# A two-block transformer kernel on one core: joined norm and logarithm steps, and fp32 one-hot products made as two fp32r parts

## The chip, the cores and the metric

The kernel runs on one core of one Trainium2 chip. The metric is the device time of one execution in microseconds (us), lower is better; several executions are timed and the median is given.

## The reference, cut to what matters

Two blocks are applied to one sequence of 256 tokens with 1024 features, all in float32. The first block runs four mixers side by side (latent attention, window means, a state-space scan, a gated recurrence), then a feed-forward part and a gated embedding. The second block has two layers: dilated attention or stick-breaking attention, each with a layer norm, a mixture of 16 experts (two per token) and another layer norm. What the change touches is this:

```python
# rmsnorm, used everywhere in the first block
y = x * rsqrt(mean(x * x, -1) + 1e-6) * g
# state-space scan: decays from running sums of a, per head
a_cs = cumsum(a, -1);  lmat = exp(segsum(a))      # segsum: a_cs[l] - a_cs[s]
# dilated attention: relative bias, a row of a 32 x 16 table per distance
bias = table[rel_bucket(dist)]
# stick-breaking attention, per head: z clipped to +-60
#   weight(i, j) = exp(z_ij - sum over j <= k < i of log(1 + exp(z_ik)))
# layer norm at the end of each of the two layers
x = (x - mean) * rsqrt(var + 1e-5) * g + b
```

## The kernel before, in words

Everything is written for a scheduler that keeps data dependences and places the instructions on the engines' queues; each engine then works its queue in order. Weights arrive by DMA on the SP queue in pieces of 128x1024 (`raw`). A piece is split into two fp32r parts: ScalarE copies it to `whi` (rounded), VectorE takes `wlo = raw - whi` (`wsplit`, L299 to L316). There are 4 buffers for each part, that is two weight pieces of 2048 columns. A projection is then three fp32r products per 128x128 weight block: `whi` by the high part of x, `whi` by its low part, `wlo` by the high part (`mm3`, called by `proj`, `proj_beside`, `proj_tok`). `sequence` and `later_pieces` list the pieces in the order of use; `piece(n)` hands out n of them and keeps one more converted ahead.

The parts that the change touches:

- `rstd` (L432): squares of x, two blocks of 128 features at a time, are added up, and a product with a matrix of ones sums over the 128 partitions. For 8 blocks the squares come as `tot` (blocks 0 to 5 added) and `sq` (the last two); with `halve` each of the two is folded to 256 columns first, so 2 products with plain fp32 operands are made; without it 4. It is called with `halve` at the start of the first block, and without it in `first_tail` (feed-forward and gated embedding) and in `dilated`.
- `rel_rows`: the rows of the relative bias come from a product of the 32x16 table with a one-hot matrix of 1152 columns, in three plain fp32 products of 384 columns.
- `ssd_dt` and `ssd`: the running sums `acs` (8 heads x 256 tokens) lie on 8 partitions; for each head a plain fp32 product with a column of the identity spreads one row over 128 partitions (8 products of 256 columns).
- `stick`: stick-breaking attention. `begin` makes the first query and key with `proj_beside`; per head `scores` clips z (`sbz`) and makes l = log(1 + exp z) (`sbl`) by Abs, Exp and Ln on ScalarE and three operations on VectorE; `sums` multiplies l (384 columns) with a triangle of ones and one 128-column part of it with ones, both in plain fp32. There are 16 heads, taken by pairs, and four quads of heads; the order of the steps is the list `steps`.
- `across_norm`: between the first expert stage and `stick`, 32 warm-up products, then 16 transposes, then per block of 128 features ScalarE makes the high part, VectorE the scaled x and the low part.
- `moe` and `token_norm`: after the last expert, the two halves of the tokens are each normed by a chain of small operations; in the second layer gain and offset rows follow and the four quarters of the output are stored.

Of the kernel before, what the change touches and what calls it, by code (L numbers as in the profile page):

```python
# [8 lines left out]
F32 = mybir.dt.float32  # L9
# [7 lines left out]
D = 1024  # L17
# [186 lines left out]
class Kern:  # L204
# [142 lines left out]
    def piece(self, n=1, beside=None):  # L347

        while len(self.made) < n + 1 and self.pieces:
# [3 lines left out]
        now, self.made = self.made[:n], self.made[n:]  # L353
        return now if n > 1 else now[0]
# [51 lines left out]
    def proj_beside(self, ws, kt, x, evacs, step):  # L406
# [3 lines left out]
        for k0 in range(0, kt, step):  # L410
# [21 lines left out]
    def rstd(self, x, nb, eps, dim, halve=False):  # L432
# [11 lines left out]
        if halve:  # L444
            for t in both:
                self.tt(t[:, 0], t[:, 0], t[:, 1], OP.add)
# [232 lines left out]
    def rel_rows(self):  # L679
# [3 lines left out]
        oh = A.tile([32, RELW], F32, name="bucket")  # L683
        nc.gpsimd.dma_start(oh, self.ap["bucket"])
# [135 lines left out]
    def first_tail(self, acc):  # L820
# [195 lines left out]
    def ssd_dt(self, src):  # L1016
# [19 lines left out]
        self.acs = A.tile([8, S], F32, name="acs")  # L1036
        nc.vector.tensor_copy(self.acs, ph[:8, :S])
        self.dtT = dt

    def ssd(self, xb):  # L1040
# [43 lines left out]
        def pair(hp):  # L1084
            o = self.ps("od")
            for s_ in range(2):
# [3 lines left out]
                self.mm(pr[:, :S], self.k["ident"][:8, h:h + 1].to_broadcast([8, 128]), self.acs, True, True)  # L1090
# [27 lines left out]
    def dtend(self):  # L1118
        t = self.A.tile([8, 8], F32, name="dend")
        self.ts(t, self.k["ident"][:8, :8], self.acs[:, 127:128], OP.mult)  # L1120
# [53 lines left out]
    def dilated(self, x, h):  # L1174
# [12 lines left out]
        def ev_q(quad, g):  # L1187
            def ev(j, p):
                nonlocal r
                if r is None:  # L1190
                    r = self.rstd(x, 8, 1e-6, D)
# [143 lines left out]
    def stick(self, x, h):  # L1335
        nc, A, ap = self.nc, self.A, self.ap
        self.table("natural_log_exp_and_others")
        self.later_pieces()
        at = self.new_split(8)
        tiles = {}  # L1340

# [6 lines left out]
        def begin():  # L1348
            self.proj_beside(self.piece(2), 8, h,
                             [ev("q", 0, 0.125), ev("k", 0, 1.0)], 2)  # L1350
# [10 lines left out]
        def scores(quad, hp):  # L1361
# [12 lines left out]
            for z, l in zip(zs, ls):  # L1374
# [6 lines left out]
            tiles["z", quad, hp] = zs, ls  # L1381

        def sums(quad, hp):

            for z, l in zip(*tiles["z", quad, hp]):
# [238 lines left out]
    def moe(self, layer, x):  # L1624
# [116 lines left out]
        def down(i, hs):  # L1741
# [4 lines left out]
            wd = wsp[1] if i == 8 else self.beside([ap["e_d"][layer, 2 * i + s] for s in range(2)], 2048)  # L1746
# [55 lines left out]
        self.raws, self.turn = raws, -1  # L1802
        across(7)
        back(*ys.pop(0), False, False)
        y = down(*prev)
# [6 lines left out]
    def token_norm(self, layer, xr, acc, along):  # L1812
# [5 lines left out]
        for n, c in enumerate(cols):  # L1818
            for t in range(2):
# [3 lines left out]
                self.act(sq, xr[:, t, c], AF.Square, accum_out=sqs[:, t, n:n + 1])  # L1823
        for t in range(2):
            o = slice(t, t + 1)
            self.tt(nm[:, o], sums[:, t, 0:1], sums[:, t, 1:2], OP.add)
            self.tt(rs[:, o], sqs[:, t, 0:1], sqs[:, t, 1:2], OP.add)
            self.ts(nm[:, o], nm[:, o], -1.0 / D, OP.mult)
            self.tt(u[:, o], nm[:, o], nm[:, o], OP.mult)
            self.stt(rs[:, o], rs[:, o], 1.0 / D, u[:, o], OP.mult, OP.subtract)  # L1830
            self.act(rs[:, o], rs[:, o], AF.Sqrt, bias=self.eps[1e-5])
            nc.vector.reciprocal(rs[:, o], rs[:, o])
            self.tt(nmr[:, o], nm[:, o], rs[:, o], OP.mult)
            for n, c in enumerate(cols):
                if n:
# [3 lines left out]
                if along:  # L1839
                    self.tt(xr[:, t, c], xr[:, t, c], along[0][:, c], OP.mult)  # L1840
                    self.tt(xr[:, t, c], xr[:, t, c], along[1][:, c], OP.add)
                    nc.sync.dma_start(self.out[t * 128:t * 128 + 128, c], xr[:, t, c])
# [154 lines left out]
```

## Time and profile before

| | us |
|---|---|
| runs shown, median (lowest to highest of 3) | 1289.57 (1289.53 to 1291.12) |
| the profiled execution, its own time | 1292.46 |
| span of the profiled execution, first to last instruction | 1290.7 |
| TensorE (PE) busy | 1258.6 |
| VectorE (DVE) busy | 731.3 |
| ScalarE (ACT) busy | 610.2 |
| mean granted TensorE clock, share of full speed | 0.991 |

The profile lists, for each engine, what it did and how long it stood idle before, and what ended the idle time. PEld is the weight load of TensorE, which runs beside the products. The chain of waits follows the work that ended last back to the start. A plain fp32 product of TensorE shows as two records; an fp32r product as one. Records of TensorE overlap, so the distance from start to start is what a product costs in a row of products. In the span, the first block takes the time to about 545 us, dilated attention to about 838 us, the first expert stage and its norm to about 994 us, stick-breaking attention to about 1123 us, the second expert stage to about 1275 us, the last norm and the store the rest.

### The profile page before, as it was taken

The page shows a single profiled execution, that of the slowest core. Times are in us where ns is not written, and L with a number is a line of the kernel's source. Part 1 is how long each engine was busy: PE and PEld are TensorE (multiplying, and loading weights), DVE is VectorE, ACT ScalarE, POOL GpSimd, SP SyncE. Part 2 cuts the span into 40 slices and gives each one's busy share as a digit, 9 for nine tenths or more (in the row PEclk, how much of TensorE's full clock was granted, in tenths as well). Part 3 has the DMA queues.
Part 4 walks back from the last instruction along what each step waited for, and adds up shares of the span by engine and source line. Part 5 has one row for each costly group of instructions (what it writes and reads, how often), then busy time and mean ns, then how long its engine had stood idle before and what let it go on. Part 6 is the DMA issues. An engine that isn't in the chain of part 4 may idle for free.

```text
span 1290.7 us, 22672 instructions
## 1 busy us (share of the span) xinstructions
PE 1258.6 (98%) x9159; PEld 1043.3 (81%) x9159; DVE 731.3 (57%) x1416; ACT 610.2 (47%) x951; POOL 24.8 (2%) x48
## 2 busy tenths in 40 slices
PE   9999999999999999999999999999998999999995
PEld 7987899999999999999999999855334999754332
DVE  7877667558665545876464646263215677454214
ACT  6674666446544544755454545232115666242112
POOL 0000000000000000000000000002000000002000
PEclk9999999999999999999999999999999999999998
DMA  7452346657486555566464645599999444557893
GB/s 263 147 183 71 109 137 204 187 178 241 142 300 229 178 186 176 185 190 187 141 194 134 194 134 170 166 318 332 358 395 370 131 131 131 191 196 272 331 397 132
DMA packets 91105, 268.28 MB, mean 208 GB/s; under 512 B 26528, under 2 KB 26672, under 8 KB 90736
## 3 DMA queue, kind: packets, MB, share of 16 engines
q1 hardware_dynamic: 86576, 252.80, 58.5%
q0 software_dynamic: 4416, 13.94, 3.2%
q8 instruction: 74, 1.21, 0.4%
q14 instruction: 39, 0.32, 0.1%
HBM read 267.68 MB, written 6.89 MB: 213 GB/s over the span
## 4 chain that ended last, share of the span: by engine, by line
PE 86%; DVE 5%; DMA 4%; ACT 3%; issue 1%; SPq 0%; ACTq 0%; DVEq 0%
PE ps L250 54%; PE acc L250 14%; PE y L250 6%; PE sc L250 4%; PE o L250 2%; PE sd L250 1%; PE o L258 1%; ACT whi L236 1%; DVE wlo L239 1%; PE sc L1265 1%; DMA raw<-e_d 1%; PE tr L250 1%; DMA s<-rows 1%; DMA wlo<-e_gu 1%; DMA raw<-e_gu 1%
## 5 line engine op out<-in xcount | busy, mean ns | idle before, releaser
L250 PE MATMUL ps<-s,whi 128*128 128x256 f32 x2656 | 495.0, 286 | 5.3 <-DVE s L239 2.5
L239 DVE TENSOR_TENSOR wlo<-raw,whi 128x1024 fp32r<-128x1024 f32 x276 | 333.8, 1218 | 258.5 <-ACT whi L236 258.0
L236 ACT ACTIVATE whi<-raw 128x1024 fp32r<-128x1024 f32 x276 | 287.1, 1054 | 307.1 <-PE ps L250 222.9
L250 PEld LDWEIGHTS ps<-s,whi 128*128 128x128 f32 x2656 | 414.9, 190 | 12.3 <-DVE s L239 4.0
L250 PE MATMUL ps<-s,wlo 128*128 128x256 f32 x1328 | 378.2, 285 | 1.3 <-DVE wlo L239 1.3
L250 PEld LDWEIGHTS ps<-s,wlo 128*128 128x128 f32 x1328 | 251.0, 189 | 4.6 <-DVE wlo L239 2.6
L250 PE MATMUL acc<-hid,whi 128*128 128x256 f32 x512 | 93.0, 281 | 0.0
L250 PE MATMUL ps<-whi,s 128*128 128x256 f32 x512 | 92.3, 282 | 0.0
L250 PE MATMUL ps<-raw,xg 128*64 128x512 f32 x344 | 86.2, 597 | 0.0
L250 PEld LDWEIGHTS ps<-whi,s 128*128 128x128 f32 x512 | 78.2, 188 | 1.5
L250 PEld LDWEIGHTS acc<-hid,whi 128*128 128x128 f32 x512 | 79.3, 189 | 0.0
L250 PE MATMUL acc<-hid,wlo 128*128 128x256 f32 x256 | 72.3, 283 | 0.0
L250 PE MATMUL ps<-wlo,s 128*128 128x256 f32 x256 | 71.7, 280 | 0.0
L250 PEld LDWEIGHTS ps<-raw,xg 128*64 128x64 f32 x344 | 25.7, 136 | 43.9 <-issue 40.5
L236 ACT ACTIVATE eh<-ps 128x256 f32<-128x256 f32 x16 | 6.2, 385 | 114.9 <-PE ps L250 114.9
L247 DVE SCALAR_TENSOR_TENSOR eh<-ps,gslot,eh 128x256 f32<-128x256 f32 x16 | 7.7, 484 | 85.2 <-ACT eh L236 85.2
L236 ACT ACTIVATE s<-y 128x512 fp32r<-128x512 f32 x36 | 21.0, 597 | 69.2 <-PE y L250 69.2
L239 DVE TENSOR_TENSOR s<-y,s 128x512 fp32r<-128x512 f32 x36 | 24.3, 686 | 50.6 <-ACT s L236 50.4
L250 PEld LDWEIGHTS ps<-wlo,s 128*128 128x128 f32 x256 | 48.1, 188 | 0.0
L250 PE MATMUL acc<-s,whi 128*128 128x256 f32 x256 | 47.7, 286 | 0.3 <-ACT dprobT L236 0.3
L250 PEld LDWEIGHTS acc<-hid,wlo 128*128 128x128 f32 x256 | 47.9, 187 | 0.0
L250 PE MATMUL y<-raw,hs 128*64 128x512 f32 x180 | 46.7, 600 | 0.0
(407 smaller groups left out, 1748.9 us busy)
## 6 DMA issues: line engine op xcount, KB each, us to landing
raw<-e_gu SPq DMA_DIRECT2D x81, 512.0 KB, 7.9
raw<-w_dil SPq DMA_DIRECT2D x72, 512.0 KB, 4.6
raw<-w_ff SPq DMA_DIRECT2D x64, 512.0 KB, 4.7
raw<-e_d SPq DMA_DIRECT2D x43, 512.0 KB, 10.1
raw<-w_g SPq DMA_DIRECT2D x32, 512.0 KB, 4.0
whi<-e_gu SPq DMA_DIRECT2D x31, 512.0 KB, 8.4
raw<-w_a SPq DMA_DIRECT2D x28, 512.0 KB, 4.8
raw<-w_sb SPq DMA_DIRECT2D x24, 512.0 KB, 7.8
```

The lines of the kernel that those rows point to most:

```text
L236: return self.nc.scalar.activation(out, in_, func, **k)
L239: return self.nc.vector.tensor_tensor(out, a, b, op=op)
L247: return self.nc.vector.scalar_tensor_tensor(out, a, s, b, op0=op0, op1=op1, **k)
L250: self.last_mm = self.nc.tensor.matmul(out, l, r, start=first, stop=last, skip_group_check=True).ins,
L258: self.nc.tensor.matmul(p, self.ones_b, r, start=True, stop=True, skip_group_check=True)
L1265: nc.tensor.transpose(pt[:, c * 128:(c + 1) * 128], e[:, order[c]], self.k["ident"])
```

## The change

- `rstd` with `halve` first adds `sq` to `tot` and folds once, so one fp32 product stands where two stood; the calls in `first_tail` and `dilated` now use `halve` too.
- `rel_rows`, `ssd` and `sums` take the data operand in two fp32r parts (a rounded copy by ScalarE, the remainder by VectorE) and multiply each with the one-hot, triangle or ones matrix in fp32r. `l` has 2 buffers in place of 6, its parts 4 each, and the `half` tiles of this stage 3 in place of 4.
- `begin` of `stick` makes all products with the high part of x first, then those with the low part.
- `token_norm` works on both halves of the tokens at once; in the second layer the mean is taken off and the gain applied while the square root is made.
- `moe` issues the last expert's down weights before the last transposes, and the list of stick weights is filled there; `make(0)` converts none.

```diff
+    def make(self, n, beside=None):
+        while len(self.made) < n and self.pieces:
...
-    def proj_beside(self, ws, kt, x, evacs, step):
+    def proj_beside(self, ws, kt, x, evacs, step, second=False):
         out = [self.ps() for _ in ws]
-        for k0 in range(0, kt, step):
+        for part in (0, 1) if second else ():
+            for k0 in range(0, kt, step):
+                for w, p in zip(ws, out):
+                    for b in range(2):
+                        for k in range(k0, min(k0 + step, kt)):
+                            for i, xp in ((0, x.lo),) if part else ((0, x.hi), (1, x.hi)):
+                                self.mm(p[:, b * S:(b + 1) * S], self.cut(w[i], k * S + b * 128, 128), xp[:, k],
+                                        not part and i == 0 and k == 0 and b == 0, part == 1 and k == kt - 1)
+        for k0 in () if second else range(0, kt, step):
...
         if halve:
-            for t in both:
-                self.tt(t[:, 0], t[:, 0], t[:, 1], OP.add)
+            if len(both) > 1:
+                self.tt(tot, tot, both.pop(), OP.add)
+            self.tt(tot[:, 0], tot[:, 0], tot[:, 1], OP.add)
...
+        tb2 = A.tile([32, 2, 16], F32R, name="reltab2")
+        self.act(tb2[:, 0], tb, AF.Copy)
+        self.tt(tb2[:, 1], tb, tb2[:, 0], OP.subtract)
...
-            self.mm(p[:16, :384], tb, oh[:, c0:c0 + 384], True, True)
+            for i in range(2):
+                self.mm(p[:16, :384], tb2[:, i], oh[:, c0:c0 + 384], i == 0, i == 1)
...
-                rs.append(self.rstd(x, 8, 1e-6, D))
+                rs.append(self.rstd(x, 8, 1e-6, D, True))
...
-        self.acs = A.tile([8, S], F32, name="acs")
-        nc.vector.tensor_copy(self.acs, ph[:8, :S])
+        self.acs = [A.tile([8, S], F32R, name=f"acs{i}") for i in range(2)]
+        self.act(self.acs[0], ph[:8, :S], AF.Copy)
+        self.tt(self.acs[1], ph[:8, :S], self.acs[0], OP.subtract)
+        self.mid, self.pick8 = A.tile([8, 1], F32, name="acs_mid"), A.tile([8, 8], F32R, name="pick8")
+        nc.vector.tensor_copy(self.mid, ph[:8, 127:128])
+        nc.vector.tensor_copy(self.pick8, self.k["ident"][:8, :8])
...
-                self.mm(pr[:, :S], self.k["ident"][:8, h:h + 1].to_broadcast([8, 128]), self.acs, True, True)
+                for i, a in enumerate(self.acs):
+                    self.mm(pr[:, :S], self.pick8[:, h:h + 1].to_broadcast([8, 128]), a, i == 0, i == 1)
...
-            ls = [A.tile([128, 384], F32, name="sbl", bufs=6) for _ in ps]
+            parts = [[A.tile([128, 384], F32R, name=n, bufs=4) for n in ("sblh", "sbll")] for _ in ps]
+            ls = [A.tile([128, 384], F32, name="sbl", bufs=2) for _ in ps]
...
+                self.act(hi, l, AF.Copy)
+                self.tt(lo, l, hi, OP.subtract)
...
-                self.mm(pr[:, :384], self.k["suffix"], l, True, False)
-                self.mm(pr[:, 128:256], self.ones, l[:, 256:384], False, True)
+                for i, l in enumerate(parts):
+                    self.mm(pr[:, :384], suffix, l, i == 0, False)
+                    self.mm(pr[:, 128:256], ones, l[:, 256:384], False, i == 1)
...
+        wd = down_weights(prev[0])
+        if not layer:
+            self.later_pieces()
+            self.make(0)
         across(7)
         back(*ys.pop(0), False, False)
-        y = down(*prev)
+        y = down(*prev, wd)
...
+        self.tt(nm, sums[:, :, 0], sums[:, :, 1], OP.add)
+        self.ts(nm, nm, -1.0 / D, OP.mult)
+        def centre(t):
+            for c in cols:
+                self.stt(xr[:, t, c], xr[:, t, c], nm[:, t:t + 1], along[0][:, c], OP.add, OP.mult)
+        if along:
+            centre(0)
+        self.tt(u, nm, nm, OP.mult)
+        self.tt(rs, sqs[:, :, 0], sqs[:, :, 1], OP.add)
+        self.stt(rs, rs, 1.0 / D, u, OP.mult, OP.subtract)
+        self.act(rs, rs, AF.Sqrt, bias=self.eps[1e-5])
+        if along:
+            centre(1)
+        nc.vector.reciprocal(rs, rs)
...
+                if along:
+                    self.stt(xr[:, t, c], xr[:, t, c], rs[:, o], along[1][:, c], OP.mult, OP.add)
+                    nc.sync.dma_start(self.out[t * 128:t * 128 + 128, c], xr[:, t, c])
```

## Rows read from the trace of the kernel before

**Rows 1.** The page, parts 1 and 4: busy time, and the chain by engine.

```profile
PE 1258.6 (98%) x9159; PEld 1043.3 (81%) x9159; DVE 731.3 (57%) x1416; ACT 610.2 (47%) x951; POOL 24.8 (2%) x48
...
PE 86%; DVE 5%; DMA 4%; ACT 3%; issue 1%; SPq 0%; ACTq 0%; DVEq 0%
```

**Rows 2.** Windows: stretch, length, busy PE, PEld, DVE, ACT, POOL, clock, DMA, GB/s.

```profile
0.00:207.00 207.00, 199.91 (x1407) 175.77 (x1408) 150.18 (x353) 130.77 (x224) 5.59 (x22) 0.98 0.48 156
...
341.00:521.00 180.00, 180.00 (x1488) 177.99 (x1487) 100.08 (x114) 86.99 (x103) 1.81 (x4) 1.00 0.62 204
...
984.00:1012.00 28.00, 25.34 (x161) 19.87 (x159) 20.93 (x49) 20.00 (x32) 0.00 (x0) 0.94 0.60 231
...
1043.00:1067.00 24.00, 24.00 (x192) 21.73 (x190) 17.16 (x37) 16.19 (x27) 0.00 (x0) 1.00 0.41 132
...
1226.00:1275.00 49.00, 48.14 (x206) 19.84 (x202) 8.09 (x15) 8.40 (x16) 0.00 (x0) 1.00 0.85 326
```

**Rows 3.** The chain of waits in order of time: start, length, what, records.

```profile
529.31 1.73 PE acc L250 x8
...
607.35 1.75 PE sc L1265 x16
...
1024.29 1.73 PE sc L250 x8
1026.03 5.76 PE ps L250 x48
```

**Rows 4.** Timeline of PE in the feed-forward part: products of `rstd`.

```profile
335.55 1.03 PE L250 MATMUL acc<-half,ones 128*128 128x256 f32 x4
```

**Rows 5.** Products by tile: the relative bias, then the state-space rows.

```profile
L250 PE MATMUL ps<-bucket,reltab x6: 481/481/492, 342.5 to 361.4; 32*16 32x384 f32 x6
...
L250 PE MATMUL sd<-acs,consts x16: 374/426/478, 101.9 to 136.3; 8*128 8x256 f32 x16
```

**Rows 6.** Timeline of PE: fp32r products of 320 columns in an expert stage.

```profile
1178.47 1.33 PE L250 MATMUL y<-oneh,s 128*128 128x320 f32 x8
...
1180.23 1.33 PE L250 MATMUL y<-oneh,s 128*128 128x320 f32 x8
```

**Rows 7.** Groups by form: DVE and ACT on 128x384 tiles of stick-breaking attention.

```profile
L236 ACT ACTIVATE sbl<-sbl 128x384 f32<-128x384 f32 x32 | 15.8, 518 | 0.5
...
L247 DVE SCALAR_TENSOR_TENSOR sbl<-sbz,sbl 128x384 f32<-128x384 f32 x16 | 8.9, 555 | 10.9 <-ACT sbl L236 10.9
```

**Rows 8.** Timeline from the end of the first expert stage into stick-breaking attention.

```profile
984.70 7.08 PE L258 MATMUL tr<-ones_b 128*128 128x512 bf16 x32
...
994.51 0.38 PE L250 MATMUL ps<-s,whi 128*128 128x256 f32 x1
...
995.36 1.36 ACT L236 ACTIVATE s<-y,vecs 128x256 fp32r<-128x256 f32 x2
...
996.08 0.39 PE L250 MATMUL ps<-s,whi 128*128 128x256 f32 x1 [1.19 <-DVE s L239]
...
997.84 0.55 PE L250 MATMUL ps<-s,whi 128*128 128x256 f32 x1 [1.14 <-DVE s L239]
...
1001.69 0.42 DVE L239 TENSOR_TENSOR s<-x,s 128x256 fp32r<-128x256 f32 x1
...
1003.37 1.06 ACT L236 ACTIVATE whi<-raw 128x1024 fp32r<-128x1024 f32 x1 [1.86 <-PE ps L250]
...
1010.49 0.40 PE L250 MATMUL ps<-whi,s 128*128 128x256 f32 x2
```

**Rows 9.** Timeline from the last expert's sums to the end.

```profile
1274.61 0.69 DVE L1820 CUSTOM_DVE_ANT_0 x<-x,acc 128x512 f32<-128x512 f32 x1 [0.28 <-PE acc L250]
...
1279.27 2.50 DVE L239 TENSOR_TENSOR x<-x,s 128x512 f32<-128x512 f32 x4
...
1282.45 2.50 DVE L239 TENSOR_TENSOR x<-x,s 128x512 f32<-128x512 f32 x4
```

**Rows 10.** Waits from 984 to 1125 us: total, times, longest.

```profile
DVE wlo L239 <- ACT whi L236: 19.9, 17, 3.4
```

More of the change, by code (lines that the diff above doesn't have):

```diff
@@ L347, in piece @@
     def piece(self, n=1, beside=None):
-        while len(self.made) < n + 1 and self.pieces:
+        self.make(n + 1, beside)
+        now, self.made = self.made[:n], self.made[n:]
+        return now if n > 1 else now[0]
+    def make(self, n, beside=None):
+        while len(self.made) < n and self.pieces:
             src, width = self.pieces.pop(0)
@@ L1190, in ev @@
                 if r is None:
-                    r = self.rstd(x, 8, 1e-6, D)
+                    r = self.rstd(x, 8, 1e-6, D, True)
                     self.table("natural_log_exp_and_others")
@@ L1337, in stick @@
         self.table("natural_log_exp_and_others")
-        self.later_pieces()
+        if self.dense:
+            self.later_pieces()
         at = self.new_split(8)
         tiles = {}
+        suffix, ones = (A.tile([128, 128], F32R, name=n) for n in ("suffix_r", "ones_r"))
+        nc.vector.tensor_copy(suffix, self.k["suffix"])
+        nc.vector.tensor_copy(ones, self.ones)
         def ev(n, quad, scale):
@@ L1370, in scores @@
             zs = [A.tile([128, 384], F32, name="sbz", bufs=6) for _ in ps]
[L1371 removed]
+            parts = [[A.tile([128, 384], F32R, name=n, bufs=4) for n in ("sblh", "sbll")] for _ in ps]
+            ls = [A.tile([128, 384], F32, name="sbl", bufs=2) for _ in ps]
             for p, z in zip(ps, zs):
                 self.ts(z, p[:, :384], 60.0, OP.min, -60.0, OP.max)
[L1374 removed]
+            for z, l, (hi, lo) in zip(zs, ls, parts):
                 self.act(l, z, AF.Abs)
@@ L1380, in scores @@
                     self.tt(l[:, c:c + 128], l[:, c:c + 128], self.k["strict_t"], OP.mult)
-            tiles["z", quad, hp] = zs, ls
+                self.act(hi, l, AF.Copy)
+                self.tt(lo, l, hi, OP.subtract)
+            tiles["z", quad, hp] = zs, parts
         def sums(quad, hp):
-            for z, l in zip(*tiles["z", quad, hp]):
+            for z, parts in zip(*tiles["z", quad, hp]):
                 pr = self.ps("sc")
-                self.mm(pr[:, :384], self.k["suffix"], l, True, False)
-                self.mm(pr[:, 128:256], self.ones, l[:, 256:384], False, True)
+                for i, l in enumerate(parts):
+                    self.mm(pr[:, :384], suffix, l, i == 0, False)
+                    self.mm(pr[:, 128:256], ones, l[:, 256:384], False, i == 1)
                 self.tt(z, z, pr[:, :384], OP.subtract)
@@ L1739, in hidden, with down_weights, down @@
             return hs
-        def down(i, hs):
+        def down_weights(i):
+            return wsp[1] if i == 8 else self.beside([ap["e_d"][layer, 2 * i + s] for s in range(2)], 2048)
+        def down(i, hs, wd=None):
             yparts.append(yparts.pop(0))
             y = yparts[0]
-            wd = wsp[1] if i == 8 else self.beside([ap["e_d"][layer, 2 * i + s] for s in range(2)], 2048)
+            wd = wd or down_weights(i)
             for n in range(2):
@@ L1823, in token_norm @@
                 self.act(sq, xr[:, t, c], AF.Square, accum_out=sqs[:, t, n:n + 1])
+        self.tt(nm, sums[:, :, 0], sums[:, :, 1], OP.add)
[12 more added lines that the diff above has]
+        nc.vector.reciprocal(rs, rs)
+        if not along:
+            self.tt(nmr, nm, rs, OP.mult)
         for t in range(2):
             o = slice(t, t + 1)
[L1826 to L1833, printed above, removed]
             for n, c in enumerate(cols):
-                if n:
+                if along:
+                    self.stt(xr[:, t, c], xr[:, t, c], rs[:, o], along[1][:, c], OP.mult, OP.add)
+                    nc.sync.dma_start(self.out[t * 128:t * 128 + 128, c], xr[:, t, c])
+                elif n:
                     self.ts(xr[:, t, c], xr[:, t, c], rs[:, o], OP.mult, nmr[:, o], OP.add)
```

17 lines of the change are left out of this document (7 added, 10 removed).

## The prediction

> **What bounds the kernel now.** I read the page first. TensorE is busy for 1258.6 of 1290.7 us and makes 86% of the chain that ended last, VectorE 5%, DMA 4%, ScalarE 3% [rows 1]. So a cheaper product counts in full wherever TensorE has no idle time, and a VectorE step counts only where the chain is on VectorE. Second, the windows, to see where that holds [rows 2]. In the feed-forward part TensorE is busy for all of 180 us, in a quad of stick-breaking attention for all of 24 us, with VectorE at 17.16 and ScalarE at 16.19 us of those 24. In the first 207 us it is busy 97%. From 984 to 1012 us, where the layer norm hands over to stick-breaking attention, it loses 2.7 us and the clock is 0.94. In the second expert stage DMA moves 326 GB/s, but TensorE loses under 1 us of 49: the transfers are started as buffers come free, so they move with TensorE when earlier stages shrink. After 1275 us only VectorE, ScalarE and the store are left. Third, the chain in order of time gives what a product costs.
>
> **The fp32 price.** Four fp32 products of 256 columns of `rstd` hold the chain for 1.73 us, 0.43 each; the fp32 products of `sums` for two heads (each 384 and 128 columns) for 1.73 us; 48 fp32r products of 256 columns take 5.76 us, 0.12 each; 16 transposes of 128 columns, each with a weight load of its own, 1.75 us, 0.109 each [rows 3]. So fp32 costs 0.43 / 0.12 = 3.6 times fp32r at 256 columns.
>
> **`rstd`, the joined norm.** In the gated embedding and in dilated attention four products on the chain become one, 1.30 us saved each. The feed-forward part has its four in two bursts of two [rows 4], the same work, so also 1.30. At the start of the first block two become one, 0.43. Sum 4.3 us. What it adds is VectorE work, one sum of 512 columns and one fold of 256 (about 1 us), in the three new places; there the row after the products is the square root and the reciprocal, and four PSUM banks let TensorE go on meanwhile. If that cover were gone, each place would lose that 1 us. I take 4.3, between 1.3 and 4.3.
>
> **`rel_rows` and `ssd`.** The bias rows are 3 fp32 products of 384 columns, the state-space rows 8 of 256 columns on 8 partitions; each shows as two records [rows 5]. By the 256-column price an fp32 product of 384 columns is 0.64 us. For fp32r of 384 columns there is no row; the nearest are the 320-column ones, 12 starting within 1.76 us, 0.147 each [rows 6], and 64 more columns by the step from 256 to 320 (0.027) give 0.175. So the bias rows save 3 x (0.64 - 0.35) = 0.9 us, and the state-space rows 8 x (0.43 - 0.24) = 1.5 us. The first stands where TensorE is full: 0.9. The second stands where it is busy 97%, among heads that alternate with VectorE and ScalarE through one PSUM bank: I take 1.3, between 0 and 1.5. The extra copies are small (32x16 and 8x256); the table is loaded in the first block already, so the ScalarE copy of it waits for nothing. They go together at nothing, at most 0.5 us where the one bank is released later.
>
> **`sums`.** Before, 0.865 us a head. After, two products of 384 columns (0.175) and two of 128. The nearest row for 128 columns with their own weights is the transpose, 0.109. So 2 x (0.175 + 0.109) = 0.57, 0.30 saved a head, 16 heads: 4.7 us. The Trainium skill, "TensorE: Matmul & The Clock Gate", section "Back-to-back issue gap", gives N / 2.4 + 2.5 ns, an estimate of 56 ns for 128 columns, though it says weight loads count at small N; by it alone the saving would be 6.4 us. The transpose row speaks against it, and I keep 4.7, between none (rival 1) and 6.1 (rival 2). Added are, per head, a ScalarE copy and a VectorE subtraction on 128x384, 0.52 and 0.55 us [rows 7]. Per quad of four heads VectorE goes to 17.2 + 2.2 = 19.4 and ScalarE to 16.2 + 2.1 = 18.3 us, in a period of about 24.0 - 1.2 = 22.8 us of TensorE: both still fit, with 3.4 us to spare. The parts are wanted one projection or more after `scores`, so the longer chain of a head is covered too. The two buffers of `sbl` are free again after the subtraction, well before the next pair of heads. The three `half` tiles: the fourth square waits for the first one's product, which is queued two pairs earlier. Nothing for both; the price if not is rival 1.
>
> **`begin` of stick-breaking attention and the norm ahead of it.** TensorE starts the first product at 994.51 us, waits 1.19 us and again 1.14 us for low parts, runs without a break only from 997.84 us, and goes over to the next piece at 1010.49 us; the last low part is ready at 1002.1 us [rows 8]. With the high parts first those two waits have another end: the high parts that two ScalarE operations from 995.36 us on make, the first of them done near 996.1 us [rows 8]. Up to 1.7 us could be gained, and as much again if the clock rises that much earlier. Against it stands that each `whi` buffer is now wanted until the last third of the 96 products, 20 products (2.4 us) ahead of the end, where before the first of them came free at 1003.37 us. The next piece is then converted just in time (1.06 us of ScalarE for each half, then VectorE). I take 1.0, between -1 and 3.4. The layer norm ahead of it stands behind 32 warm-up products that hold TensorE until 991.8 us [rows 8], so a shorter chain of small steps shows only in the second half of the tokens: 0.4, between -0.5 and 1.0. The four down-weight transfers moved ahead of the last transposes pass no other transfer on SP, whose next are the stick weights, and POOL issues none there; filling the list with `make(0)` starts nothing. Both: nothing.
>
> **The last norm.** From 1274.61 us VectorE has four sums (2.5 us), then two chains of small steps, then in the gaps two scalings and eight gain and offset operations, and ends at 1282.45 + 2.50 = 1284.95 us [rows 9]. After, it has the four sums, six small steps (some 0.13 each) and eight operations of 128x512 at 0.62: 1274.6 + 2.5 + 0.8 + 5.0 = 1282.9, and 0.2 for the wait on the squares. 1.8 us saved, between 1.2 and 2.1; the four stores follow each other at the same distance as the operations.
>
> **Sum.** 4.3 + 0.9 + 1.3 + 4.7 + 1.0 + 0.4 + 1.8 = 14.4 us. The profiled execution took 1292.46 us (span 1290.7 and 1.8 around it) and would take 1278.1; it lies 2.9 us above the median shown, 1289.57, and against that the sum gives 1275.2 us.
>
> **The rivals.**
> 1. Stick-breaking attention does not pay. The pieces are already converted by a relay in which VectorE waited 17 times for ScalarE, 19.9 us in all, at most 3.4 [rows 10]; the two new operations a head stand in the same queues, and a part that is late stops TensorE. For it: VectorE at 85% of the new period. Against: the longest of these waits cost TensorE nothing before. Price: the 4.7 of `sums` and the 1.0 of `begin`, 1280.9 us.
> 2. A 128-column product is not held by its weight load but streams, as the step from 320 to 256 columns would give (0.12 - 2 x 0.027 = 0.066). Then 32 products save 0.04 each: 1.4 us more, 1273.8 us. [...] The trace has the transposes against it, and they are not fp32r products.
> 3. The change does not do what it says: at 384 columns, or with 8 or 32 rows, two fp32r products cost as much as one fp32. Then 0.9 + 1.3 + 4.7 go: 1282.1 us. Against: 320 columns at 0.147.
> 4. Slower: in stick-breaking attention every piece comes late. If ScalarE's new copy stands in its queue waiting for VectorE's masks while the next `whi` stands behind it, each of some ten pieces can lose the longest wait of the relay, 3.4 us [rows 10]: 34 us against 14.4, 1309 us. It decides from 1.4 us a piece. Against: 3.4 us to spare per quad, and a piece is wanted 5.76 us after its buffer is free.
>
> **The numbers.** The forecast 0.67, rival 1 0.17, rival 2 0.06, rival 3 0.05, rival 4 0.05. A measurement of this kernel tells 0.2%, 2.6 us, from no change. All but rival 4 are faster by more, unless rivals 1 and 3 meet other losses (0.04); rival 4 in part gives another 0.01 of no change. So faster 0.91, same 0.05, slower 0.04. The low ends of the forecast's terms together (3.0 less of `rstd`, 1.3 of `ssd`, 2.0 of `begin`, 0.9 of the norm ahead of it, 0.6 of the end) are 7.8 us, 1283.0; they have little to do with each other, so the range stops at 1281.5, which takes in rival 1 and leaves out rivals 3 and 4. The high ends (`begin` 2.4, the norm 0.6, the state-space rows 0.2, the end 0.3, rival 2 1.4) are 4.9 us, so it begins at 1270.5.
>
> **What would show it.** Right: the chain has one product of 0.43 where it had 1.73 in the gated embedding and dilated attention; `sums` holds TensorE for about 1.15 us per pair; a quad is shorter by 1.2 us with TensorE full; VectorE ends about 8.3 us after its first sum of the last norm. Wrong: idle time of TensorE ended by `wlo` or `whi` between 1000 and 1110 us (rivals 1 and 4); 0.066 or 0.2 and more per 128-column product (rivals 2 and 3); a `begin` that no longer flows into the next piece; a state-space stretch that is as long as before.

## The result and the profile after

| | before | after |
|---|---|---|
| median of the runs, us | 1290.09 (1289.53 to 1291.12) | 1276.24 (1275.38 to 1277.45) |
| ratio after / before, with its 95% interval | | 0.989 (0.9875 to 0.991) |
| profiled execution, span, us | 1290.7 | 1273.5 |

The kernel became 13.9 us faster, where 14.4 us were forecast. The sum came out nearly right, but four of its terms did not, in both directions. The page of the kernel after, parts 1 and 4, answers to [rows 1]: TensorE lost 15 us of busy time, VectorE gained 7 and is still far from being the bound. (In the title only the norm's steps are joined; those of the logarithm are the same as before, and the two parts of its result are what is new.)

```profile
PE 1243.3 (98%) x9139; PEld 1035.6 (81%) x9139; DVE 738.0 (58%) x1426; ACT 613.6 (48%) x965; POOL 24.8 (2%) x48
...
PE 85%; DMA 6%; DVE 4%; ACT 3%; issue 2%; SPq 0%; DVEq 0%; ACTq 0%
```

The windows after (columns as in [rows 2]) show the hand-over to stick-breaking attention and a quad. From 984 to 1012 us, now cut at another place of the work, the clock is 1.00 where it was 0.94; in the 23.0 us of a window inside a quad TensorE is busy throughout, with VectorE at 19.1 and ScalarE at 17.8. By the starts in the chain a whole quad takes 24.31 us before and 23.14 after.

```profile
984.00:1012.00 28.00, 25.88 (x207) 23.98 (x206) 21.36 (x41) 19.76 (x31) 0.00 (x0) 1.00 0.54 192
...
1032.00:1055.00 23.00, 23.00 (x193) 21.77 (x192) 19.12 (x41) 17.81 (x33) 0.00 (x0) 1.00 0.46 137
```

The chain of waits after (start, length, what) answers to [rows 3]: the products of `rstd` in the gated embedding and in dilated attention take 0.43 to 0.47 us in place of 1.73, and `sums` of two heads 1.10 in place of 1.73, with the next projection right behind.

```profile
525.15 0.47 PE acc L250 x2
...
556.25 0.43 PE sc L250 x2
...
1014.69 1.10 PE sc L250 x8
1015.78 5.80 PE ps L250 x48
```

**Where the time went.** Both chains pass through the same pieces of work, so the start of one piece, before and after, gives what each stretch lost. Stretches are safer than medians here: executions of one kernel differ by 2 us and more, and what makes them differ lies in a few places (waits of about 1 us in the expert stages, and the clock in the first block, last section). The two starts in the first block, 210.54 and 208.70 us in the chain, are 1.84 us apart, but that is one of these places and not the change, as experiment 5 shows.

| stretch, by the pieces of the chain | before, us | after, us | saved | forecast |
|---|---|---|---|---|
| start to the first weights after the first `rstd` (36.20 and 36.05) | 36.20 | 36.05 | 0.15 | 0.43 |
| state-space heads, first row product to last | 34.4 | 32.9 | 1.5 | 1.5 |
| what is left of both at the end of the first block (experiment 5) | | | 0.1 to 0.4 | 1.7 |
| feed-forward, up to the products at 354.78 and 351.67 | 144.24 | 142.97 | 1.27 | 1.30 |
| the next, with the bias rows (to 367.88 and 363.82) | 13.10 | 12.15 | 0.95 | 0.9 |
| to the first product after the gated embedding's `rstd` (531.04, 525.62) | 163.16 | 161.80 | 1.36 | 1.30 |
| from there to the end of dilated attention's `rstd` | 31.15 | 31.06 | 0.09 | 1.30 |
| last down products to the first product of `begin` | 16.19 | 16.54 | -0.35 | 0.4 |
| `begin` to the end of the first quad | 23.83 | 20.90 | 2.93 | 1.0 |
| three quads and the end of stick-breaking attention | 108.92 | 104.21 | 4.71 | 4.7 |
| the last norm, first sum to last operation of VectorE | 10.34 | 8.81 | 1.53 | 1.8 |

With 0.3 for the first block together 12.8 us, against 13.9 between the medians; the rest is no more than the runs scatter. The table leaves two stretches out: from the end of dilated attention's `rstd` to the last down products, and from the end of stick-breaking attention to the last norm, which hold the two expert stages. They are 1.5 and 1.4 us shorter in the profile after, but among the eleven profiles with the change (this one and those of the ten runs below) they differ by 2.8 and 2.0 us, with the kernel before inside that spread. The first row is no clear saving either: in those eleven profiles that start lies between 35.95 and 36.26 us, before at 36.20. Four rows ask for an experiment: the lost 1.3 us in dilated attention, the lost state-space rows, the layer norm that became longer, and the 2.9 us of `begin`.

### The profile page after: what moved, and what is told of

Read it like the earlier page. It is cut to its first block, busy times and chain, and to the rows that moved or that the text cites. A ratio compares the mean times of both kernels' runs of the same rounds, so it can differ in the third digit from the quotient of the medians.

```text
span 1273.5 us, 22652 instructions
## 1 busy us (share of the span) xinstructions
PE 1243.3 (98%) x9139; PEld 1035.6 (81%) x9139; DVE 738.0 (58%) x1426; ACT 613.6 (48%) x965; POOL 24.8 (2%) x48
## 4 chain that ended last, share of the span: by engine, by line
PE 85%; DMA 6%; DVE 4%; ACT 3%; issue 2%; SPq 0%; DVEq 0%; ACTq 0%
PE ps L250 54%; PE acc L250 13%; PE y L250 5%; PE sc L250 4%; PE o L250 2%; DMA raw<-e_gu 2%; DMA raw<-w_sb 1%; PE o L258 1%; PE sd L250 1%; DVE wlo L239 1%; PE sc L1287 1%; DMA raw<-e_d 1%; ACT whi L236 1%; PE tr L250 1%; DMA wlo<-e_gu 1%
```

## The experiments

Each kernel is the changed one with one edit; begin_filled has that of begin_mixed and one more, joined3 has three, again none. They ran in three groups, each beside the kernel before, to which the ratio is taken: the first four of the table, the next four, the last two.

| run | median, us | ratio to before |
|---|---|---|
| dil_bank | 1274.19 | 0.9875 (0.9857 to 0.9893) |
| begin_mixed | 1279.63 | 0.9919 (0.9901 to 0.9937) |
| sums_whole | 1281.06 | 0.9932 (0.9914 to 0.9951) |
| norm_apart | 1277.82 | 0.9910 (0.9890 to 0.9930) |
| begin_filled | 1280.02 | 0.9907 (0.9888 to 0.9926) |
| hi_first | 1277.66 | 0.9893 (0.9874 to 0.9912) |
| rows_whole | 1279.76 | 0.9908 (0.9888 to 0.9927) |
| no_ones | 1274.40 | 0.9871 (0.9851 to 0.9890) |
| joined3 | 1273.33 | 0.9867 (0.9848 to 0.9887) |
| again (the changed kernel) | 1275.86 | 0.9891 (0.9872 to 0.9910) |

**1. The 1.3 us of dilated attention.** At the hand-over from the gated embedding to dilated attention the timeline of the kernel after shows TensorE idle for 1.59 us, ended by VectorE's reading of the last gated piece:

```profile
543.66 0.68 DVE L239 TENSOR_TENSOR half<-ps,rstd 128x512 f32<-128x512 f32 x1
...
544.49 0.48 PE L250 MATMUL ps<-s,whi 128*128 128x256 f32 x2 [1.59 <-DVE half L239]
```

In the trace before, 13 products of dilated attention ran ahead of this point. The two programs as built give out the PSUM banks of the feed-forward part in another order (the trace leaves the numbers out): before, the last gated piece lay in bank 2, after, it lies in bank 0, and the next stage's first tile is in bank 0 in both. So I gave bank 0 to a tile that is needed later:

```diff
         with self.psum(name, ps=3, sc=4, o=1):
+            if name == "dil":
+                self.ps("o")
             for do, *of in steps:
```

> The changed kernel, with the PSUM banks of the dilated stage shifted by one, so that its first two tiles lie in banks that the gated embedding gave up two and more pieces earlier. Theory (the 1.3 us of `rstd` in dilated attention were saved and lost again, because in the changed kernel the first tile of dilated attention fell into the bank of the last gated piece): the idle time of TensorE at the hand-over falls from 1.59 us to 0.3 to 0.6 us, and the stretch from the first product after the gated embedding's `rstd` to the end of dilated attention's `rstd` falls from 31.06 us to about 30.0; the whole is 1.0 us shorter, about 1275.2. Rival (the next products wait for VectorE's low parts of x in any case): idle time stays over 1.2 us, the stretch at 31.0, the time at 1276.2.

The timeline of dil_bank: TensorE waits 0.34 us, for a low part of x, as in the kernel before.

```profile
546.50 0.39 PE L250 MATMUL ps<-s,whi 128*128 128x256 f32 x1 [0.34 <-DVE s L247]
```

The stretch is 557.19 - 527.33 = 29.86 us in place of 31.06. The theory holds: the cheaper `rstd` did save 1.3 us, and the order of the banks, which the change had moved as a side effect, took them back. (The median is 2.0 us lower, more than the stretch; it comes from another group of runs.)

**2. `begin` of stick-breaking attention.** The two waits of [rows 8] against one. The old order of its products alone:

```diff
-                             [ev("q", 0, 0.125), ev("k", 0, 1.0)], 2, True)
+                             [ev("q", 0, 0.125), ev("k", 0, 1.0)], 2)
```

> The changed kernel, with the products of `begin` of stick-breaking attention in the old order (high and low part of x in turn). Theory (the waits for low parts also kept TensorE's clock down): the stretch from the first product of stick-breaking attention to the end of its first quad, 20.9 us in the changed kernel and 23.8 before, goes back to 23.5 to 24, and the granted clock in the first 14 us of it falls under 0.95 again; the time is 2.9 us longer, about 1279.1. Rival 1 (waits alone): the stretch is 22 to 22.5 us at a clock of 1.00, about 1277.6. Rival 2 (the gain comes from the norm ahead of it and the earlier weights): it stays at 21 us, 1276.2.

The stretch goes back to 1012.99 - 989.21 = 23.78 us and the time to 1279.63. The timeline of begin_mixed shows the two waits for low parts, and what follows them: the pair of products at 993.25 takes 0.40 us, the pair at 994.21 takes 0.63.

```profile
990.80 0.38 PE L250 MATMUL ps<-s,whi 128*128 128x256 f32 x1 [1.20 <-DVE s L239]
...
992.56 0.39 PE L250 MATMUL ps<-s,whi 128*128 128x256 f32 x1 [1.14 <-DVE s L239]
...
993.25 0.40 PE L250 MATMUL ps<-s,whi 128*128 128x256 f32 x2
...
994.21 0.63 PE L250 MATMUL ps<-s,whi 128*128 128x256 f32 x2
```

The window from 992 to 999 us of the same run has a clock of 0.76:

```profile
992.00:999.00 7.00, 6.44 (x41) 6.44 (x42) 4.67 (x11) 3.61 (x4) 0.00 (x0) 0.76 0.04 15
```

From about 993.8 to 997 us products follow each other at 0.21 us in place of 0.12: TensorE is at the lower of its two levels, 1.2 GHz, after two waits of over a microsecond with three products between them. In the changed kernel one wait of 1.20 us is left, and the clock stays at 1.00. To see what the waiting costs and what the clock, I filled the two waits with products that nothing reads:

```diff
-                        self.mm3(p[:, b * S:(b + 1) * S], w, k * S + b * 128, 128,
-                                 x, lambda t: t[:, k], k == 0 and b == 0, k == kt - 1)
+                        for i, xp in ((0, x.hi), (0, x.lo), (1, x.hi)):
+                            self.mm(p[:, b * S:(b + 1) * S], self.cut(w[i], k * S + b * 128, 128), xp[:, k],
+                                    k == 0 and b == 0 and i == 0 and xp is x.hi, k == kt - 1 and i == 1)
+                            if fill and k == 0 and b == 0 and p is out[0] and i == 0 and xp is x.hi:
+                                self.warm("o", fill)
+                        if fill and k == 0 and b == 0 and p is out[0]:
+                            self.warm("o", fill)
```

> The kernel of the run begin_mixed, with ten products of a constant (0.22 us each, into a bank that nothing reads) put into TensorE's queue, five after the first and five after the third product of `begin`, where it stood idle for 1.20 and 1.14 us. Theory (half of what the old order costs is waiting, half is the clock that falls after the two waits): the waits are as long as before but filled, the granted clock of the first 14 us stays at 1.00, the stretch from the first product to the end of the first quad is 22.4 us (23.8 without the filling), the time 1278.2. Rival (the clock falls whatever stands in the gaps, or is not what costs): the stretch stays at 23.6 to 23.9 us, the time at 1279.6.

The timeline of begin_filled, and one window of it:

```profile
990.15 1.25 PE L258 MATMUL o<-ones_b 128*128 128x512 bf16 x5
991.53 0.39 PE L250 MATMUL ps<-s,whi 128*128 128x256 f32 x1
...
991.87 1.25 PE L258 MATMUL o<-ones_b 128*128 128x512 bf16 x5
```

```profile
993.00:1000.00 7.00, 6.94 (x57) 6.70 (x56) 5.75 (x12) 4.81 (x5) 0.00 (x0) 1.00 0.02 8
```

The clock stays at 1.00 and the stretch is 1012.30 - 989.93 = 22.37 us: of the 2.9 us the clock is 1.4, and the waiting (with the new order) 1.5. The median did not follow (1280.02 against 1279.63): the profile of this run has a wait of 1.25 us in the second expert stage, ended by VectorE's `gslot`, that begin_mixed has not. The four kernels of this group of runs all show it (1.20 to 1.25 us); of the other profiles only that of the kernel before has it (1.18). So the stretch decides here and the median does not.

The wait that is left in `begin`, after its second product, is for a high part: ScalarE makes the blocks in the order 0, 2, 4, 1, 3. I wrote all high parts ahead of VectorE's work:

```diff
+        blocks = []
         for b in range(8):
...
             self.act(hi, src, AF.Identity, scale=g, bias=o)
+            blocks.append((dst, src, g, o))
+        for b, (dst, src, g, o) in enumerate(blocks):
             self.ts(dst, src, g, OP.mult, o, OP.add)
             self.tt(sp.lo[:, b], y[:, b], sp.hi[:, b], OP.subtract)
```

> The changed kernel, with all eight high parts of `across_norm` written ahead of VectorE's work, so that ScalarE makes them in the order of the blocks (in the changed kernel it takes blocks 0, 2, 4, 1, 3). Theory (the one wait that is left in `begin`, 1.20 us after its second product, is for the second block's high part, which ScalarE makes fourth): the wait falls under 0.3 us and the stretch from the first product of stick-breaking attention to the end of its first quad goes from 20.9 to about 19.9 us; the time is 1.0 us shorter, 1275.2. Rival (VectorE's low parts, now later, or the next weight pieces take its place): TensorE waits as much further on in `begin`, and the time stays at 1276.2.

The timelines, first of the changed kernel, then of hi_first:

```profile
989.54 0.38 PE L250 MATMUL ps<-s,whi 128*128 128x256 f32 x1 [1.20 <-ACT s L236]
```

```profile
989.31 2.50 ACT L236 ACTIVATE s<-y,vecs 128x256 fp32r<-128x256 f32 x4 [0.97 <-PE y L1898]
...
990.74 0.38 PE L250 MATMUL ps<-s,whi 128*128 128x256 f32 x1
```

The stretch is 1009.92 - 990.17 = 19.75 us, 1.15 less. The median is again hidden by the wait in the expert stage (and by 1.5 us of the clock in the first block, below); it is paired in the last run.

**3. `sums`.** Back to plain fp32, without parts:

```diff
-                self.act(hi, l, AF.Copy)
-                self.tt(lo, l, hi, OP.subtract)
...
-                for i, l in enumerate(parts):
-                    self.mm(pr[:, :384], suffix, l, i == 0, False)
-                    self.mm(pr[:, 128:256], ones, l[:, 256:384], False, i == 1)
+                self.mm(pr[:, :384], self.k["suffix"], l, True, False)
+                self.mm(pr[:, 128:256], self.ones, l[:, 256:384], False, True)
```

> The changed kernel, with `sums` of stick-breaking attention in plain fp32 again, without the two parts. Theory (the products are the whole of the gain, and the copy and the subtraction lie beside TensorE's work): a pair's products take 1.73 us in place of 1.10, a quad 24.3 us in place of 23.2, the time is 4.7 us longer, about 1280.9. Rival (VectorE and ScalarE are near the bound, and without their added 4.3 us a quad the other work flows better): the time is under 3.5 us longer, with TensorE's idle time in the quads lower than in the changed kernel.

The chain of sums_whole, and the window of one of its quads:

```profile
1015.16 1.73 PE sc L250 x8
1016.90 5.76 PE ps L250 x48
```

```profile
1033.00:1057.00 24.00, 24.00 (x194) 21.75 (x190) 17.35 (x36) 15.91 (x27) 0.00 (x0) 1.00 0.43 132
```

A quad is 1032.67 - 1008.36 = 24.31 us, the time 4.8 us longer. TensorE is full in both. Over the second quad of each, VectorE is busy for 19.27 us in the changed kernel and 17.48 here, ScalarE for 17.96 and 16.22; these added 1.8 and 1.7 us lie beside TensorE's work and cost nothing. How the 1.10 us of a pair divide shows when the products of 128 columns are left out:

```diff
                 for i, l in enumerate(parts):
-                    self.mm(pr[:, :384], suffix, l, i == 0, False)
-                    self.mm(pr[:, 128:256], ones, l[:, 256:384], False, i == 1)
+                    self.mm(pr[:, :384], suffix, l, i == 0, i == 1)
```

> The changed kernel without the 32 products of 128 columns with the matrix of ones in `sums` of stick-breaking attention: the later half of the keys is left out of the sums of the earlier half. Theory (behind a product of 384 columns they stream at the 0.06 us that lie between their starts and the next): a quad is 0.48 us shorter, the time 1.9 us, 1274.3. Rival (each is held by its weight load as a transpose is, 0.109 us): a quad is 0.87 us shorter, the time 3.5 us, 1272.7.

The chain of no_ones:

```profile
1015.90 0.71 PE sc L250 x4
1016.61 5.76 PE ps L250 x48
```

Four products of 384 columns are 0.71 us, 0.178 each; the four of 128 were the other 0.39, 0.098 each. A quad is 1032.41 - 1009.96 = 22.45 us, 0.69 less than in the changed kernel, which is 0.087 for each of its eight. Over the rest of stick-breaking attention (104.21 us in the changed kernel, 1111.20 - 1009.96 = 101.24 here) it is 0.093 each. Both theories missed, the rival by less: in the timeline after, a 128-column product starts only 0.06 us ahead of the next one, but leaving it out saves 0.087 to 0.098. (The median agrees with the theory only by the wait of 1.23 us in the expert stage that this group has.)

**4. The norm.** The old `token_norm` in both layers (the removed lines of the diff above put back):

> The changed kernel, with the old `token_norm` in both layers (each half of the tokens by itself). Theory (the joined form pays at the end and costs a little in the first layer, where the four low-part conversions stand between its small steps): from VectorE's first sum to its last operation of the last norm 10.3 us in place of 8.8, and in the first layer from the last expert's down products to the first product of stick-breaking attention 16.2 us in place of 16.5; together 1.2 us longer, about 1277.4. Rival (the first layer is late because of the moved weights, not of the norm): that stretch stays at 16.5 us, and the time is 1.5 us longer, 1277.7.

In the first layer the stretch is 987.92 - 971.74 = 16.18 us, and in the last norm 1269.03 - 1258.68 = 10.35 us: the theory on both counts. The moved weights, which norm_apart keeps, cost nothing in the first stretch (16.19 before). The timeline of the kernel after shows why joining costs in the first layer: one `tn_b` for both halves of the tokens stands behind two conversions of stick's weights that VectorE's queue has between the small steps, and ScalarE begins to scale x only then.

```profile
981.91 1.23 DVE L239 TENSOR_TENSOR wlo<-raw,whi 128x1024 fp32r<-128x1024 f32 x1 [0.32 <-DMA raw<-w_sb]
...
983.06 0.16 DVE L1875 RECIPROCAL tn_r<-tn_r 128x2 f32<-128x2 f32 x1
983.13 1.21 DVE L239 TENSOR_TENSOR wlo<-raw,whi 128x1024 fp32r<-128x1024 f32 x1
984.25 0.15 DVE L239 TENSOR_TENSOR tn_b<-tn_m,tn_r 128x2 f32<-128x2 f32 x1
...
984.50 1.52 ACT L236 ACTIVATE x<-x,tn_b,tn_r 128x512 f32<-128x512 f32 x2 [0.54 <-DVE tn_b L239]
```

In norm_apart, as in the kernel before, the first half's `tn_b` stands ahead of the second of those conversions, so that ScalarE starts 12.75 us after the down products, here 13.20.

The last norm of the kernel after answers to [rows 9]: eight operations of VectorE where two scalings and eight gain and offset operations stood, 0.67 us from start to start.

```profile
1261.90 1.42 DVE L247 SCALAR_TENSOR_TENSOR x<-x,tn_m,s 128x512 f32<-128x512 f32 x2
...
1264.96 2.74 DVE L247 SCALAR_TENSOR_TENSOR x<-x,tn_r,s 128x512 f32<-128x512 f32 x4
```

**5. The rows of biases and decays.** Both in plain fp32 again:

```diff
-            for i in range(2):
-                self.mm(p[:16, :384], tb2[:, i], oh[:, c0:c0 + 384], i == 0, i == 1)
+            self.mm(p[:16, :384], tb, oh[:, c0:c0 + 384], True, True)
...
-                for i, a in enumerate(self.acs):
-                    self.mm(pr[:, :S], self.pick8[:, h:h + 1].to_broadcast([8, 128]), a, i == 0, i == 1)
+                self.mm(pr[:, :S], self.k["ident"][:8, h:h + 1].to_broadcast([8, 128]), self.acs, True, True)
```

> The changed kernel, with the rows of the relative biases and of the state-space decays in plain fp32 products again. Theory (both stand on TensorE's path): the stretch up to the end of the first feed-forward pieces with the bias rows is 0.95 us longer there, the first block to the first piece after the state-space heads 1.3 us longer; the time is 2.2 us longer, 1278.4. Rival (the state-space heads wait for VectorE and ScalarE, and the products are hidden there): only the 0.95 us of the bias rows show, 1277.2.

The products of the state-space rows by tile (durations, first and last start), of the kernel after and of rows_whole:

```profile
L250 PE MATMUL sd<-acs,pick x16: 273/328/380, 100.2 to 133.1; 8*128 8x256 f32 x16
```

```profile
L250 PE MATMUL sd<-acs,consts x16: 374/426/478, 100.4 to 134.8; 8*128 8x256 f32 x16
```

TensorE's timeline further on, again of the kernel after and of rows_whole, where products wait for low parts of weights:

```profile
175.72 0.39 PE L250 MATMUL ps<-s,wlo 128*128 128x256 f32 x1 [0.94 <-DVE wlo L239]
...
190.96 0.38 PE L250 MATMUL ps<-s,wlo 128*128 128x256 f32 x1 [1.17 <-DVE wlo L239]
```

```profile
175.90 0.38 PE L250 MATMUL ps<-s,wlo 128*128 128x256 f32 x1 [0.95 <-DVE wlo L239]
```

In the heads the products themselves cost what was expected: from a row's first record to the start of the product behind it, the eight rows take 4.99 us in rows_whole and 3.42 in the kernel after. (The stretches of 34.4 and 32.9 us differ by as much only by chance; the second holds eight projection products fewer.) This saving is carried on. At the wait just ahead of these lines, for a high part of weights (it ends at 174.28 and at 174.45 us), TensorE has 12 products more behind it in the kernel after, and when 1290 products are done it stands at 188.80 us there and at 190.40 in rows_whole, 1.60 ahead.

It is lost at 190.96 us, in the wait of 1.17 us for the low part of a weight piece. rows_whole and the kernel before have no such wait; the ten other profiles, all with the rows in two parts, have it (1.15 to 1.17). VectorE's timeline, of the kernel after and of rows_whole, shows why: that low part (the 46th that VectorE makes) stands behind ten operations of the window means (`row`, `a4p`) in the one and ahead of them in the other.

```profile
184.33 1.22 DVE L239 TENSOR_TENSOR wlo<-raw,whi 128x1024 fp32r<-128x1024 f32 x1
185.47 0.42 DVE L239 TENSOR_TENSOR row<-a4p,a 128x256 f32<-128x256 f32 x1
...
189.68 1.22 DVE L239 TENSOR_TENSOR wlo<-raw,whi 128x1024 fp32r<-128x1024 f32 x1
```

```profile
186.17 1.22 DVE L239 TENSOR_TENSOR wlo<-raw,whi 128x1024 fp32r<-128x1024 f32 x1
187.30 0.42 DVE L239 TENSOR_TENSOR row<-a4p,a 128x256 f32<-128x256 f32 x1
...
191.52 1.22 DVE L239 TENSOR_TENSOR wlo<-raw,whi 128x1024 fp32r<-128x1024 f32 x1
```

The ones product of the next `rstd` starts at 208.74 us in rows_whole, against 208.57 in the kernel after: 0.17 is left. Whether the old order in VectorE's queue would keep the 1.5 us is not shown; no run changed that order alone. The comparison with the kernel before must be made between profiles with the same clock in this block (last section): there the product starts at 210.41 before and at 210.01 to 210.27 in four kernels with the change (dil_bank, begin_mixed, hi_first, joined3), so 0.14 to 0.40 us is what both terms of the first block left.

From there on the bias rows are as forecast: from the scores at 208.86 us to the products after the bias rows at 364.93 it is 156.07 us, in the kernel after 155.12, 0.95 less. The rival holds in the size, not in its reason: the products are on TensorE's path, and what they free is lost in a wait that comes with the changed order of VectorE's queue. The whole run came out 3.5 us slower than the kernel after, more than these rows account for: its profile has waits of 1.23, 1.06 and 1.07 us in the expert stages, of the kind named under begin_filled.

**6. The three mends together**, with the changed kernel beside it in the same group of runs. The edits are those of dil_bank and hi_first, and the old `token_norm` where no gain and offset rows follow:

```diff
+        if not along:
+            return self.apart(xr, sums, sqs, nm, rs, nmr, u, cols)
         self.tt(nm, sums[:, :, 0], sums[:, :, 1], OP.add)
```

> The changed kernel with three mends: the banks of dilated attention shifted (as in dil_bank), the high parts of across_norm first (as in hi_first), and the old small steps of the norm in the first layer alone. Theory (the three places are independent and lie on TensorE's path): TensorE's idle time at the hand-over 0.3 us in place of 1.6, the stretch of `begin` and the first quad 19.75 us in place of 20.9, from the down products to `begin` 16.2 us in place of 16.5; together 2.7 us under the changed kernel beside it, about 1273.6. Rival (the second expert stage waits for its weights, so what is gained ahead of it is lost there): under 1.5 us shorter, with more idle time of TensorE ended by a transfer after 1113 us.

> The changed kernel once more, as the measure for the one beside it, and to see how the granted clock in the first block stands in another execution of the same program. Theory (the clock between 68 and 76 us falls in some executions and not in others, whatever the kernel, and costs 1.5 us): the time is 1276.2 within 1.5 us; where the clock falls, the first 211 us are 1.5 us longer than in the first profile of it. Rival (the fall belongs to some kernels): the first block is as in the first profile, 208.7 us to the first scores after the state-space heads.

joined3 took 1273.33 us (1271.6 to 1275.0), the changed kernel beside it 1275.86 (1275.1 to 1277.85): 2.5 us less, against 2.7 expected, so the gains add up and the second expert stage did not take them back. It is the fastest of the kernels that leave nothing out. Its timeline has the hand-over and the first product of `begin`:

```profile
545.94 0.39 PE L250 MATMUL ps<-s,whi 128*128 128x256 f32 x1 [0.34 <-DVE s L247]
...
987.05 0.38 PE L250 MATMUL ps<-s,whi 128*128 128x256 f32 x1
```

From the down products (970.86) to `begin` it is 16.19 us, from there to the end of the first quad (1006.74) 19.69.

## Why the prediction was right, and where not

- **fp32 price, `sums`, bias rows: right.** 3.6 times fp32r at 256 columns held: 0.865 us a head became 0.55, forecast 0.57, and the division into 0.175 and 0.109 was measured as 0.178 and 0.087 to 0.098. Rival 2 (0.066 us for 128 columns) and rival 3 (no gain at 384 columns) fell. The Trainium skill, "TensorE: Matmul & The Clock Gate", section "Back-to-back issue gap", gives about 56 ns for 128 columns by its formula, says that this leaves out the weight load, and gives about 81 ns as measured in a stream. The 87 to 98 ns here lie nearer to the second figure; that the weight load is the reason is not shown by a run.
- **VectorE and ScalarE beside a quad: right.** Forecast 19.4 and 18.3 us in 22.8; measured 19.3 and 18.0 in a quad of 23.1 with TensorE full. (The forecast took the 24.0 us of a window for the quad, which is 24.31; the 1.2 us that come off it were right.) Rivals 1 and 4 fell with it: no wait of TensorE for a weight part between 1000 and 1110 us.
- **`rstd`, 4.3 us: 2.9 measured.** "Four PSUM banks let TensorE go on meanwhile" was true of the square root and the reciprocal, but I did not look at which bank the next stage begins in. The product itself fell from 1.73 to 0.43 us in dilated attention, and 1.2 us came back as idle time at the hand-over, by the bank (dil_bank). At the start of the first block the 0.43 did not show: VectorE's reciprocal behind the products starts at 19.05 us before and 19.08 after. At the end of that block 0.1 to 0.4 us is left of this term and the next one together.
- **State-space rows, 1.3 us: 0.4 at most.** The saving of 1.5 us in the heads came as forecast. "The second stands where it is busy 97%" was the step that failed: it took the waits of the block as given, but the changed program has another order in VectorE's queue, and with it a wait of 1.17 us that the old one has not (rows_whole).
- **`begin`, 1.0 us: 2.9.** The two parts named, the waits and the clock, were 1.5 and 1.4 us (begin_mixed, begin_filled); what I set against them, the weight buffers that come free later, cost nothing that the trace shows: the profile after shows no wait of TensorE between 990 and 1112 us. I chose the value from the mean of a gain and a loss where the rows of the trace bore out the gain alone.
- **Layer norm ahead of it, 0.4 us: -0.35.** The sign was wrong: the shorter chain of small steps is shorter only where it is a chain. In the first layer four conversions stand among its steps, and joining made the first half of the tokens wait for the second (norm_apart).
- **Last norm, 1.8 us: 1.5.** The mechanism was right; the eight operations with two operands and a scalar take 0.67 us each, not the 0.62 of the two-operand form.

The errors, -1.4 (`rstd`), -1.2 (state-space rows), -0.75 (first layer's norm) and -0.3 (last norm) on one side and +1.9 (`begin`) on the other, left a sum of 12.8 us where 14.4 were forecast. The measured 13.9 is nearer to the forecast than the terms deserve.

## What to carry to other kernels

A cheaper product counts in full only if no wait behind it takes the gain back: before adding up savings, list every wait of the bound engine further down the same stage, after the change see whether a conversion that it needs has slipped behind other work in its engine's queue, and for each hand-over of PSUM which bank the last tile leaves and which one the next stage asks for first. Joining small steps of two halves pays where nothing stands between them in the queue, and costs where the joined step must wait for the later half. An idle gap of the bound engine can cost twice: in `begin` two gaps of over 1 us cost 1.5 us as waiting and order and 1.4 us as clock, and filling them with products that nothing reads saved the second part.

## What was not expected of the hardware

**The granted clock in the first block falls in some executions of one and the same program.** Around 66.7 us TensorE waits 1.06 us and then makes products of 8 columns. The window from 68 to 76 us of the changed kernel, first in its first profile, then in the run again:

```profile
68.00:76.00 8.00, 8.00 (x67) 7.53 (x67) 7.89 (x15) 6.76 (x11) 0.27 (x2) 1.00 0.45 139
```

```profile
68.00:76.00 8.00, 8.00 (x56) 6.90 (x55) 6.45 (x11) 5.32 (x10) 0.26 (x2) 0.81 0.33 93
```

Eleven records fewer in the same 8 us: by the next wait, at 174.28 and 175.72 us, the fall has cost 1.4 us. There the second place of this kind lies: after two waits of 0.80 and 0.94 us the clock is 0.94 over 170 to 200 us in the first profile and 1.00 in the run again. That makes up the 1.4 us by 180 us; a wait of 0.69 us for VectorE at 187.95, which the first profile has not, takes half of it back (the ones product starts at 208.57 and 209.31 us). So over the first 211 us the fall cost 0.7 us, not the 1.5 that were expected of the run again. Of the twelve profiles, seven have the first fall and five have not, the kernel before with it and the first profile of the kernel after without: this is the 1.84 us between their first blocks, which look like the 1.7 that were forecast. Without the other profiles I would have counted the state-space rows as a hit.

**A product's distance to the next start is not its price here.** Behind 384 columns the 128-column product starts 0.06 us ahead of its successor, and 0.087 to 0.098 us go when it is left out.
